# Summing the squares of three of the four RMS norms: on VectorE in SBUF, or on TensorE in PSUM

## The chip, the cores and the metric

One core of a Trainium2 chip runs the whole kernel. The metric is the device time of one execution in microseconds (us); the times are the median of three runs. The profile and the trace are those of one profiled execution.

## The reference

A decoder trunk of two layers over 256 tokens (T) and 2048 channels (D), all in f32. Layer 0 mixes by sliding-window attention, layer 1 by a gated linear recurrence (HGRN2). Both then run a squared-ReLU MLP of width 8192. There are four RMS norms over the channels, each followed by a shift and a scale from a conditioning vector:

```python
def rms_norm(x, gain):
    y = xf * lax.rsqrt(jnp.mean(xf * xf, axis=-1, keepdims=True) + EPS)
    return (y * gain.astype(jnp.float32)).astype(x.dtype)
...
    h = modulate(rms_norm(x, norm_mix[i]), sh1, sc1)
    ...
    x = x + g1[:, None, :] * y
    h = modulate(rms_norm(x, norm_mlp[i]), sh2, sc2)
    x = x + g2[:, None, :] * squared_relu_mlp(h, mlp_w1[i], mlp_w2[i])
```

## The kernel before, in words

**Layout.** The residual x lives in SBUF turned on its side: 16 blocks `X[kb]` of 128 channels (partitions) by 256 tokens. Each block is 128x256 f32. So the sum of squares of one token runs over all partitions of all 16 blocks.

**Matmuls.** Weights come in tiles of 1 MB (`raw`, five buffers, loaded by SyncE's queue at L212). ScalarE casts each half tile to a high part `wh` (L237), and VectorE subtracts to get the low part `wl` (L238), five buffers each. So up to four half tiles can be ready ahead of the one that TensorE is using. Activations are split in the same way into high and low parts. TensorE multiplies high by high, high by low and low by high. A product over 2048 channels is therefore 32 matmuls (two of 512 and 256 columns per block) or 48 (three of 256 columns per block, the "fold" form and the form `u`). All TensorE instructions are recorded at one line, L50, so they are told apart by their tiles: `mm` is a product, `ss` a sum of squares.

**The conditioning vectors.** The shifts, scales and gates are matrix-vector products. VectorE does most of them: one instruction per 1 MB tile at L226 (`raw<-raw,cond`), in an order that a list `seq` sets when the kernel is built, mixed with the weight tiles.

**The norms.** Norm one, at the start, runs over x as loaded. Norm two (before the MLP of layer 0), norm three (before the recurrence) and norm four (before the MLP of layer 1) run while the 16 blocks of x are being made: each time a block is ready (`resid` at L566 in attention and recurrence output, L942 in the last quarter of an MLP), `finish_x` puts a call of `norm_add` in a list of background work, and a `hook` between the matmuls calls it some matmuls later. `norm_add` squares the block on ScalarE (L470) into a tile `w` (three buffers), and later TensorE sums it over the partitions with a 32-column weight of ones. The four groups of 32 partitions of the PSUM tile `ss` take every fourth block. `pep` pins these matmuls behind the TensorE instruction in front of them. After the sixteenth, ScalarE copies `ss` to SBUF (L480).

**The end of a norm.** `norm_rstd` sums the copied tile over its partitions with two one-column matmuls (`sst`, with the column `quad` that is one in every 32nd row). It takes the reciprocal root on VectorE with small `nsm` instructions (L130 to L136, L492) and makes a diagonal `dg` (L497). `norm_bcast` spreads it over the partitions with one matmul `rb`, and ScalarE copies it to `rbs` (L505). Only then can `make_h` (L532 to L537) make the normed blocks H. Between x's last block and H, TensorE works on products of the not yet normed x (`u`, made at L549 to L551; the norm is multiplied in afterwards at L1008). At norms three and four there are three such products (`start_phase`), at norm two a larger number (`open_mlp`).

**Order.** A scheduler orders each engine's instructions when the kernel is built. On the chip each engine works through its own list in that order.

Of the kernel before, what the change touches and what calls it, by code (L numbers as in the profile page):

```python
# [7 lines left out]
F32 = mybir.dt.float32  # L8
F32R = mybir.dt.float32r
I32 = mybir.dt.int32  # L10
AF = mybir.ActivationFunctionType
ALU = mybir.AluOpType
AX = mybir.AxisListType

P = 128
T = 256
D = 2048
KB = 16
# [19 lines left out]


class Queue:  # L40
    """TensorE, with the name of its latest instruction; pinned instructions are issued behind that one."""

    def __init__(self, tc, engine, last, pin):
        self.tc, self.engine, self.last, self.pin = tc, engine, last, pin
# [17 lines left out]
def trunk(ctx, tc, a, out):  # L62
    nc = tc.nc
    dve, act, sp, pool_q = nc.vector, nc.scalar, nc.sync, nc.gpsimd
    last = []
    pe, pep = Queue(tc, nc.tensor, last, False), Queue(tc, nc.tensor, last, True)
# [4 lines left out]
    tmp = ctx.enter_context(tc.tile_pool(name="tmp", bufs=2))  # L71
    psum = ctx.enter_context(tc.tile_pool(name="psum", bufs=1, space=bass.MemoryType.PSUM))
# [5 lines left out]
    X = [xt[k // 4][:, k % 4, :] for k in range(KB)]  # L78
    col = iter(range(0, NCST))

    def part(n):
        c = next(col)
        for _ in range(n - 1):
            next(col)
        return cst[:, c:c + n]
# [4 lines left out]
    quad, kq, ogain = part(1), part(2), part(HG)  # L90
# [4 lines left out]
    ones = const.tile([P, P], F32, tag="ones", name="ones")  # L95
# [33 lines left out]
    def rsqrt(v, y, t, b):  # L129
        dve.tensor_scalar(out=y.bitcast(I32), in0=v.bitcast(I32), scalar1=-0.5,  # L130
                          scalar2=float(0x5F3759DF), op0=ALU.mult, op1=ALU.add)
        dve.tensor_scalar(out=b, in0=v, scalar1=-0.5, scalar2=None, op0=ALU.mult)
        for _ in range(3):
            dve.tensor_tensor(out=t, in0=y, in1=y, op=ALU.mult)
            dve.tensor_tensor(out=t, in0=t, in1=b, op=ALU.mult)
            dve.scalar_tensor_tensor(out=y, in0=t, scalar=1.5, in1=y, op0=ALU.add, op1=ALU.mult)  # L136
# [169 lines left out]
    def later(delay, fn):  # L306
        bg.append((bgst["slot"] + delay, bgst["n"], fn))
        bgst["n"] += 1
        bg.sort(key=lambda e: (e[0], e[1]))
# [144 lines left out]
    def wt(cols=T, name="w"):  # L454
        return tmp.tile([P, cols], F32, tag="w", name=name, bufs=3)
# [9 lines left out]

    nstate = {}

    def norm_add(kb, delay=0):
        sq = wt()
        act.activation(out=sq, in_=X[kb], func=AF.Square)  # L470
        if kb == 0:
            nstate["ss"] = psum.tile([P, T], F32, tag="pv", name="ss", bufs=1)
        g = slice((kb % 4) * 32, (kb % 4 + 1) * 32)

        def add():
            (pep if delay else pe).matmul(nstate["ss"][g, :], lhsT=ones[:, :32], rhs=sq,
                                          start=(kb < 4), stop=(kb >= 12))
            if kb == KB - 1:
                nstate["sc"] = wt()
                act.copy(out=nstate["sc"], in_=nstate["ss"])  # L480
        if delay:
            later(delay, add)
        else:
            add()

    def norm_rstd():
        ss = psum.tile([P, 2], F32, tag="sm", name="sst", bufs=1)
        for b in range(2):
            pe.matmul(ss[:, b:b + 1], lhsT=nstate["sc"][:, b * P:(b + 1) * P], rhs=quad,
                      start=True, stop=True)  # L490
        sm = tmp.tile([P, 8], F32, tag="nsm", name="nsm")
        dve.tensor_scalar(out=sm[:, 0:2], in0=ss, scalar1=1.0 / D, scalar2=EPS,  # L492
                          op0=ALU.mult, op1=ALU.add)
        rsqrt(sm[:, 0:2], sm[:, 2:4], sm[:, 4:6], sm[:, 6:8])
        dg = tmp.tile([P, T], F32, tag="dg", name="dg", bufs=1)
        for b in range(2):
            dve.tensor_scalar(out=dg[:, b * P:(b + 1) * P], in0=ident, scalar1=sm[:, 2 + b:3 + b],  # L497
                              scalar2=None, op0=ALU.mult)
        nstate["dg"] = dg

    def norm_bcast():
        rb = psum.tile([P, T], F32, tag="sm", name="rb", bufs=1)
        pe.matmul(rb, lhsT=ones, rhs=nstate["dg"], start=True, stop=True)
        rbs = tmp.tile([P, T], F32, tag="rbs", name="rbs", bufs=1)
        act.copy(out=rbs, in_=rb)  # L505
        return rbs

    def norm_finish():
        norm_rstd()
        return norm_bcast()  # L510

    gsc = const.tile([P, 4, KB], F32, tag="gsc", name="gsc")
# [33 lines left out]
    def make_u(l, half, kb):  # L546
        g = gsc[:, l * 2 + half, kb:kb + 1]
        u = optile(sets[0], kb)
        act.activation(out=u[:, :T], in_=X[kb], func=AF.Copy, scale=g)  # L549
        act.copy(out=u[:, T:T + 2], in_=ustate["sw"][:, kb, :].bitcast(F32))  # L550
        dve.scalar_tensor_tensor(out=u[:, T + 2:], in0=X[kb], scalar=g, in1=u[:, :T].bitcast(F32),  # L551
                                 op0=ALU.mult, op1=ALU.subtract)
        return u
# [15 lines left out]
    def evac_res(l, which, n):  # L569
        def f(ps):  # L570
            resid(l, which, n, ps)
            finish_x(n)
        return f
# [3 lines left out]
    def finish_x(n):  # L577
        if ustate["next"] is not None and n < ustate["lim"]:
            ustate["U"][n] = make_u(*ustate["next"], n)
        if n < KB - 1:  # L580
            later(2, lambda: norm_add(n, 2))
        elif ustate["next"] is None:
            norm_add(n)

    # layer 0: norm and modulation
    for k in range(KB):
        norm_add(k)
    rbs = norm_finish()
    feed = Feed(0, 0, rbs)
    feed.need(KH)  # L590
    H = feed.H
    ahead(LAG - 1)

    # layer 0: attention
    O = [None] * KB
    with tc.tile_pool(name="attn", bufs=2) as ap:
        dist = ap.tile([P, T], F32, tag="dist", name="dist", bufs=1)
# [239 lines left out]
    def open_mlp(mp, A, relu2):  # L837
# [5 lines left out]
        for n in range(2):  # L843
            finish_x(n)
# [10 lines left out]
        def s1():  # L855
            norm_rstd()
            later(NB, s2)
# [49 lines left out]
    def mlp_layer(l, H, last):  # L907
        mp_name = f"mlp{l}"
        with tc.tile_pool(name=mp_name, bufs=1) as mp:
# [20 lines left out]
            def evac2(c, n, fold):  # L930
                def f(ps):
                    if c == 0:
                        acc_tile(n)
                        total(ps, acc[n])
                        return
                    if not fold:
                        t = wt()
                        act.copy(out=t, in_=ps[:, T:])  # L938
                        dve.tensor_tensor(out=acc[n], in0=acc[n], in1=t, op=ALU.add)  # L939
                    dve.tensor_tensor(out=acc[n], in0=ps[:, :T], in1=acc[n], op=ALU.add)  # L940
                    if c == NCHUNK - 1:
                        dve.scalar_tensor_tensor(  # L942
                            out=X[n], in0=acc[n], scalar=mods[:, l, G2 * 16 + n: G2 * 16 + n + 1],
                            in1=X[n], op0=ALU.mult, op1=ALU.add)
                        if last:
                            act.dma_start(out=out[n], in_=X[n])
                        else:
                            finish_x(n)
                return f
# [32 lines left out]
    def start_phase(l, half, count, alloc, sink):  # L982
# [12 lines left out]
        def s1():  # L995
            norm_rstd()
            later(NB, s2)
# [21 lines left out]

    mlp_layer(0, None, False)  # L1020

    # layer 1: HGRN2
    hpool = ctx.enter_context(ExitStack())
    hp = hpool.enter_context(tc.tile_pool(name="hgrn", bufs=1))
    cmask = hp.tile([P, T], I32, tag="cmask", name="cmask")
# [281 lines left out]
```

## Time and profile before

| | |
|---|---|
| median of 3 runs | 2361.89 us (2360.89 to 2362.2) |
| span of the profiled execution | 2360.6 us, 1.3 us under the median |
| TensorE busy (matmuls) | 2294.6 us, 97% |
| VectorE busy | 1804.8 us, 76% |
| ScalarE busy | 1166.0 us, 49% |
| mean granted TensorE clock | 0.988 |
| HBM | 253 GB/s over the span |

The page gives busy times by engine, 40 slices of the span, the chain of work that ended last and the costliest groups of instructions. The profiled execution has no time of its own beside its span. In rows of the timeline the first number is the start in us, the second the duration. A number in square brackets at the end is the idle time of the engine in front of the row, and what ended it.

### The profile page before, as it was taken

To read this page: it belongs to the slowest core of one execution; us is meant where nothing else is said; L and a number is where in the kernel's file an instruction comes from. 1 tells how busy PE (TensorE), PEld (TensorE's weight loads), DVE (VectorE), ACT (ScalarE), POOL (GpSimd) and SP (SyncE) were. 2 spreads that over 40 slices of the span, in tenths; PEclk is the share of its full clock that TensorE was granted. 3 is DMA by queue.
4 is the path that set the end of the run, shared out by engine and by line. 5 is a ranking of instruction groups with operands and counts; after the bars stand their busy time and mean duration, and the time that the engine had idled before them with its cause. 6 is when DMAs were issued, how large, how long until landed. Compare 5 with 4: busy or idle time off the path is not lost.

```text
span 2360.6 us, 36968 instructions
## 1 busy us (share of the span) xinstructions
PE 2294.6 (97%) x14634; PEld 1992.4 (84%) x14634; DVE 1804.8 (76%) x3016; ACT 1166.0 (49%) x1977; POOL 3.5 (0%) x10
## 2 busy tenths in 40 slices
PE   2989999999999999999999999999999999999999
PEld 0985589998888888887888998999888888888888
DVE  8898777866888988986998888755865766665665
ACT  2435744544444444454665666644544444444443
POOL 0000000000000000000000000000000000000000
PEclk6999999999999999999999999999999999999999
DMA  9987788556989889874587777544666666555552
GB/s 381 339 307 305 285 322 322 192 187 241 322 333 338 322 325 336 320 289 161 198 299 257 265 268 268 196 158 160 219 229 235 248 216 249 198 194 181 194 191 95
DMA packets 84638, 598.80 MB, mean 254 GB/s; under 512 B 9456, under 2 KB 11504, under 8 KB 12272
## 3 DMA queue, kind: packets, MB, share of 16 engines
q1 hardware_dynamic: 81936, 593.81, 69.9%
q8 instruction: 115, 1.88, 0.3%
q10 hardware_dynamic: 2304, 2.10, 0.3%
q0 software_dynamic: 224, 0.52, 0.1%
q14 instruction: 59, 0.48, 0.1%
HBM read 594.04 MB, written 2.10 MB: 253 GB/s over the span
## 4 chain that ended last, share of the span: by engine, by line
PE 95%; DVE 3%; ACT 1%; DMA 1%; issue 0%; SPq 0%; ACTq 0%
PE mm L50 89%; DVE raw L226 2%; PE ss L50 1%; PE S L50 1%; PE A L50 1%; PE pv L50 1%; PE pt L50 1%; DVE wl L238 1%; PE on L50 0%; DMA raw<-in_mod_w_dram 0%; DMA x<-in_x_dram 0%; ACT wh L237 0%; DVE ht L532 0%; PE ssq L50 0%; PE sst L50 0%
## 5 line engine op out<-in xcount | busy, mean ns | idle before, releaser
L238 DVE TENSOR_TENSOR wl<-raw,wh 128x1024 fp32r<-128x1024 f32 x744 | 906.7, 1222 | 436.4 <-ACT wh L237 434.6
L237 ACT CAST wh<-raw 128x1024 fp32r<-128x1024 f32 x744 | 779.2, 1051 | 927.1 <-PE mm L50 836.6
L50 PE MATMUL mm<-h,wh 128*128 128x512 f32 (+2 forms) x3728 | 1154.1, 368 | 37.1 <-ACT wh L237 37.1
L50 PE MATMUL mm<-h,wl 128*128 128x256 f32 (+1 forms) x3232 | 907.0, 281 | 7.6 <-DVE wl L238 7.6
L50 PE MATMUL mm<-o,wh 128*128 128x512 f32 (+2 forms) x3120 | 863.1, 346 | 0.0
L50 PEld LDWEIGHTS mm<-h,wh 128*128 128x128 f32 x3728 | 671.4, 190 | 167.6 <-ACT wh L237 37.8
L50 PE MATMUL mm<-o,wl 128*128 128x256 f32 (+1 forms) x2432 | 679.6, 280 | 0.0
L50 PEld LDWEIGHTS mm<-h,wl 128*128 128x128 f32 x3232 | 612.5, 190 | 10.0 <-DVE wl L238 8.5
L50 PEld LDWEIGHTS mm<-o,wh 128*128 128x128 f32 x3120 | 538.1, 188 | 93.0 <-issue 10.4
L50 PEld LDWEIGHTS mm<-o,wl 128*128 128x128 f32 x2432 | 458.3, 189 | 0.4
L226 DVE CUSTOM_DVE_ANT_0 raw<-raw,cond 128x2048 f32<-128x2048 f32 x164 | 374.1, 2284 | 13.9 <-DMA raw<-in_mod_w_dram 10.4
L50 PE MATMUL mm<-wh,h 128*128 128x256 f32 x576 | 105.0, 283 | 1.3 <-ACT h L536 1.1
L50 PEld LDWEIGHTS mm<-wh,h 128*128 128x128 f32 x576 | 88.8, 189 | 2.2 <-ACT h L536 1.4
L50 PE MATMUL mm<-wl,h 128*128 128x256 f32 x288 | 81.0, 281 | 0.0
L459 ACT COPY w<-mm 128x256 f32<-128x256 f32 x186 | 67.6, 364 | 0.0
L463 ACT CAST h<-w 128x256 fp32r<-128x256 f32 x125 | 49.9, 404 | 28.9 <-DVE w L919 28.4
L50 PEld LDWEIGHTS mm<-wl,h 128*128 128x128 f32 x288 | 54.2, 188 | 0.5 <-issue 0.4
L919 DVE SCALAR_TENSOR_TENSOR w<-w 128x256 f32<-128x256 f32 x125 | 52.0, 421 | 2.2
L464 DVE TENSOR_TENSOR h<-w,h 128x256 fp32r<-128x256 f32 x125 | 51.5, 417 | 0.0
L460 DVE TENSOR_TENSOR w<-mm,w 128x256 f32<-128x256 f32 x109 | 45.5, 417 | 0.4 <-ACT w L459 0.2
L939 DVE TENSOR_TENSOR acc<-acc,w 128x256 f32<-128x256 f32 x94 | 39.4, 419 | 8.1 <-ACT w L938 8.0
L940 DVE TENSOR_TENSOR acc<-mm,acc 128x256 f32<-128x256 f32 x96 | 40.5, 422 | 6.5 <-PE mm L50 4.0
(193 smaller groups left out, 1113.2 us busy)
## 6 DMA issues: line engine op xcount, KB each, us to landing
raw<-in_mod_w_dram SPq DMA_DIRECT2D x164, 1024.0 KB, 5.9
raw<-in_mlp_dram SPq DMA_DIRECT2D x128, 1024.0 KB, 5.0
raw<-in_hin_dram SPq DMA_DIRECT2D x64, 1024.0 KB, 5.0
raw<-in_mlp1b_dram SPq DMA_DIRECT2D x64, 1024.0 KB, 4.9
raw<-in_mlp1a_dram SPq DMA_DIRECT2D x48, 1024.0 KB, 6.5
raw<-in_mod_g_dram SPq DMA_DIRECT2D x28, 1024.0 KB, 6.5
raw<-in_aout_dram SPq DMA_DIRECT2D x16, 1024.0 KB, 6.7
raw<-in_m1h_dram SPq DMA_DIRECT2D x16, 1024.0 KB, 4.9
```

Of the source, the lines that this page charges most:

```text
L50: r = fn(*args, **kw)
L226: dve.tensor_tensor_reduce(out=r, in0=r, in1=cond, scale=1.0, scalar=0.0, op0=ALU.mult, op1=ALU.add, accum_out=mods[:, e[1], e[2]:e[2] + 1])
L237: act.copy(out=wh, in_=part)
L238: dve.tensor_tensor(out=wl, in0=part, in1=wh.bitcast(F32), op=ALU.subtract)
L459: act.copy(out=t, in_=ps[:, T:])
L460: dve.tensor_tensor(out=out_t, in0=ps[:, :T], in1=t, op=ALU.add)
L463: act.copy(out=opt[:, :T], in_=src_t)
L464: dve.tensor_tensor(out=opt[:, T:2 * T], in0=src_t, in1=opt[:, :T].bitcast(F32), op=ALU.subtract)
L919: dve.scalar_tensor_tensor(out=t, in0=t, scalar=0.0, in1=t, op0=ALU.max, op1=ALU.mult)
L939: dve.tensor_tensor(out=acc[n], in0=acc[n], in1=t, op=ALU.add)
L940: dve.tensor_tensor(out=acc[n], in0=ps[:, :T], in1=acc[n], op=ALU.add)
```

## The change

For norms two to four, `norm_add` no longer uses TensorE. The square of block 0 is written by ScalarE straight into a tile `ssum` of 128x256 f32, in the slot of the tag `rbs`. Each of the other 15 blocks is squared into `w` as before, and VectorE adds it to `ssum`. At the end the two `sst` matmuls sum `ssum` over all its 128 rows, with a column of ones instead of `quad`. PSUM tile `ss`, its 48 matmuls and the three copies at L480 are gone from these norms. Norm one keeps its matmuls (`norm_first`); its copy goes to the tag `rbs` as well. Lines move down by two: L566 is L568, L532 is L534, L537 is L539, L497 is L499.

```diff
-    def norm_add(kb, delay=0):
+    def norm_add(kb):
+        if kb == 0:
+            nstate["ss"] = tmp.tile([P, T], F32, tag="rbs", name="ssum", bufs=1)
+            act.activation(out=nstate["ss"], in_=X[kb], func=AF.Square)
+            return
         sq = wt()
         act.activation(out=sq, in_=X[kb], func=AF.Square)
-        if kb == 0:
-            nstate["ss"] = psum.tile([P, T], F32, tag="pv", name="ss", bufs=1)
-        g = slice((kb % 4) * 32, (kb % 4 + 1) * 32)
-
-        def add():
-            (pep if delay else pe).matmul(nstate["ss"][g, :], lhsT=ones[:, :32], rhs=sq,
-                                          start=(kb < 4), stop=(kb >= 12))
-            if kb == KB - 1:
-                nstate["sc"] = wt()
-                act.copy(out=nstate["sc"], in_=nstate["ss"])
-        if delay:
-            later(delay, add)
-        else:
-            add()
+        dve.tensor_tensor(out=nstate["ss"], in0=nstate["ss"], in1=sq, op=ALU.add)
...
-    def norm_rstd():
+    def norm_rstd(sumcol=ones[:, :1]):
...
-            pe.matmul(ss[:, b:b + 1], lhsT=nstate["sc"][:, b * P:(b + 1) * P], rhs=quad,
+            pe.matmul(ss[:, b:b + 1], lhsT=nstate["ss"][:, b * P:(b + 1) * P], rhs=sumcol,
...
-            later(2, lambda: norm_add(n, 2))
+            later(2, lambda: norm_add(n))
```

TensorE in norm four, at the border between two products of the recurrence's output (`o` are the activations); before:

```order
L50 MATMUL mm<-o_15871,wh 128x256 x2
L50 MATMUL mm<-o_15871,wl 128x256
L50 MATMUL mm<-o_15884,wh 128x256 x2
L50 MATMUL mm<-o_15884,wl 128x256
L50 MATMUL ss<-w,ones 32x256
L50 MATMUL mm<-o_11910,wh 128x256 x2
L50 MATMUL mm<-o_11910,wl 128x256
```

The same place now:

```order
L50 MATMUL mm<-o_15863,wh 128x256 x2
L50 MATMUL mm<-o_15863,wl 128x256
L50 MATMUL mm<-o_15876,wh 128x256 x2
L50 MATMUL mm<-o_15876,wl 128x256
L50 MATMUL mm<-o_11902,wh 128x256 x2
L50 MATMUL mm<-o_11902,wl 128x256
```

The product's last matmul is now followed directly by the next product's first; the order around it is otherwise the same.

VectorE in norm four, one step of the same stretch (`x` is the residual, `h` the low part of `u`); before:

```order
L566 SCALAR_TENSOR_TENSOR x_74<-mm,mods,x_74 128x256
L238 TENSOR_TENSOR wl<-raw,wh 128x1024
L551 SCALAR_TENSOR_TENSOR h_16115<-x_74,gsc,h_16115 128x256
L238 TENSOR_TENSOR wl<-raw,wh 128x1024
L566 SCALAR_TENSOR_TENSOR x_74<-mm,mods,x_74 128x256
```

The same step now:

```order
L568 SCALAR_TENSOR_TENSOR x_74<-mm,mods,x_74 128x256
L238 TENSOR_TENSOR wl<-raw,wh 128x1024
L553 SCALAR_TENSOR_TENSOR h_16105<-x_74,gsc,h_16105 128x256
L486 TENSOR_TENSOR ssum<-ssum,w 128x256
L238 TENSOR_TENSOR wl<-raw,wh 128x1024
L568 SCALAR_TENSOR_TENSOR x_74<-mm,mods,x_74 128x256
```

The added instruction stands behind `h` and ahead of the second `wl`.

VectorE at the end of norm three, from the diagonal `dg` to the second normed block (`fl` are the first results of the recurrence's products, `ht` the first step of H); before:

```order
L497 TENSOR_SCALAR dg<-cst,nsm 128x128 x2
L238 TENSOR_TENSOR wl<-raw,wh 128x1024
L1008 TENSOR_TENSOR fl<-mm,rbs 128x256
L532 SCALAR_TENSOR_TENSOR ht<-x_73,gsc,rbs 128x256
L1009 TENSOR_SCALAR fl<-fl,swc 128x256
L532 SCALAR_TENSOR_TENSOR ht<-x_73,gsc,rbs 128x256
L368 TENSOR_REDUCE swc<-mm 128x1
L1008 TENSOR_TENSOR fl<-mm,rbs 128x256
L537 SCALAR_TENSOR_TENSOR h_11220<-ht,mods,h_11220 128x256
L1009 TENSOR_SCALAR fl<-fl,swc 128x256
L532 SCALAR_TENSOR_TENSOR ht<-x_73,gsc,rbs 128x256
L537 SCALAR_TENSOR_TENSOR h_11225<-ht,mods,h_11225 128x256
```

The same place now:

```order
L499 TENSOR_SCALAR dg<-cst,nsm 128x128 x2
L368 TENSOR_REDUCE swc<-mm 128x1
L238 TENSOR_TENSOR wl<-raw,wh 128x1024
L1008 TENSOR_TENSOR fl<-mm,rbs 128x256 x2
L1009 TENSOR_SCALAR fl<-fl,swc 128x256 x2
L534 SCALAR_TENSOR_TENSOR ht<-x_73,gsc,rbs 128x256 x2
L238 TENSOR_TENSOR wl<-raw,wh 128x1024
L226 ISA raw,mods<-raw,cond 128x2048
L226 ISA mods 128x1
L1060 TENSOR_SCALAR fl<-fl,om,lb 128x256 x2
L539 SCALAR_TENSOR_TENSOR h_11212<-ht,mods,h_11212 128x256
L1062 TENSOR_SCALAR kk<-fl 128x512
```

One more `wl`, one matrix-vector product (L226) and two instructions of L1060 now stand ahead of the first `h`. Between the `sst` matmuls and `dg` there are three `wl` now and two before. At the ends of norms two and four the orders of TensorE are the same but for the missing `ss` and one place of `sst`.

More of the change, by code (lines that the diff above doesn't have):

```diff
@@ L466, in trunk, with norm_first @@
     nstate = {}
-    def norm_add(kb, delay=0):
+    def norm_first():
+        ss = psum.tile([P, T], F32, tag="pv", name="ss", bufs=1)
+        for kb in range(KB):
+            sq = wt()
+            act.activation(out=sq, in_=X[kb], func=AF.Square)
+            g = slice((kb % 4) * 32, (kb % 4 + 1) * 32)
+            pe.matmul(ss[g, :], lhsT=ones[:, :32], rhs=sq, start=(kb < 4), stop=(kb >= 12))
+        nstate["ss"] = tmp.tile([P, T], F32, tag="rbs", name="ssum", bufs=1)
+        act.copy(out=nstate["ss"], in_=ss)
+        return norm_finish(quad)
+    def norm_add(kb):
+        if kb == 0:
+            nstate["ss"] = tmp.tile([P, T], F32, tag="rbs", name="ssum", bufs=1)
+            act.activation(out=nstate["ss"], in_=X[kb], func=AF.Square)
+            return
         sq = wt()
         act.activation(out=sq, in_=X[kb], func=AF.Square)
-        if kb == 0:
-            nstate["ss"] = psum.tile([P, T], F32, tag="pv", name="ss", bufs=1)
-        g = slice((kb % 4) * 32, (kb % 4 + 1) * 32)
-        def add():
-            (pep if delay else pe).matmul(nstate["ss"][g, :], lhsT=ones[:, :32], rhs=sq,
-                                          start=(kb < 4), stop=(kb >= 12))
-            if kb == KB - 1:
-                nstate["sc"] = wt()
-                act.copy(out=nstate["sc"], in_=nstate["ss"])
-        if delay:
-            later(delay, add)
-        else:
-            add()
-    def norm_rstd():
+        dve.tensor_tensor(out=nstate["ss"], in0=nstate["ss"], in1=sq, op=ALU.add)
+    def norm_rstd(sumcol=ones[:, :1]):
         ss = psum.tile([P, 2], F32, tag="sm", name="sst", bufs=1)
         for b in range(2):
-            pe.matmul(ss[:, b:b + 1], lhsT=nstate["sc"][:, b * P:(b + 1) * P], rhs=quad,
+            pe.matmul(ss[:, b:b + 1], lhsT=nstate["ss"][:, b * P:(b + 1) * P], rhs=sumcol,
                       start=True, stop=True)
@@ L506, in norm_bcast, with norm_finish @@
         return rbs
-    def norm_finish():
-        norm_rstd()
+    def norm_finish(sumcol):
+        norm_rstd(sumcol)
         return norm_bcast()
@@ L580, in finish_x @@
         if n < KB - 1:
-            later(2, lambda: norm_add(n, 2))
+            later(2, lambda: norm_add(n))
         elif ustate["next"] is None:
             norm_add(n)
-    for k in range(KB):
-        norm_add(k)
-    rbs = norm_finish()
+    rbs = norm_first()
     feed = Feed(0, 0, rbs)
```

## Prediction

> **What bounds the kernel now.** I read the page first: busy times, slices, chain.
>
> ```profile
> span 2360.6 us, 36968 instructions
> PE 2294.6 (97%) x14634; PEld 1992.4 (84%) x14634; DVE 1804.8 (76%) x3016; ACT 1166.0 (49%) x1977; POOL 3.5 (0%) x10
> PE   2989999999999999999999999999999999999999
> DVE  8898777866888988986998888755865766665665
> PE 95%; DVE 3%; ACT 1%; DMA 1%; issue 0%; SPq 0%; ACTq 0%
> ```
>
> After the first two slices TensorE has no free tenth, and the chain is 95% TensorE. VectorE is at 76% on the average but at 8 or 9 in many slices. So what leaves TensorE counts in full, unless VectorE or a transfer comes in its way there. The span is 1.3 us under the median of the runs, 2361.89; I carry the difference over to that median.
>
> Next, where the removed matmuls stand: the tile ss by stages (one window for each of norms two, three and four), then TensorE's own order of time in norm four.
>
> ```profile
> 250.00:450.00 200.00, 9.29 (x32) 2.06 (x32) 0.37 (x1) 1.00 0.78 284
> 1000.00:1200.00 200.00, 9.90 (x32) 2.20 (x32) 0.37 (x1) 1.00 0.64 228
> 1500.00:1700.00 200.00, 9.53 (x32) 2.21 (x32) 0.37 (x1) 1.00 0.50 174
> ```
>
> ```profile
> 1570.88 0.28 PE L50 MATMUL mm<-o,wl 128*128 128x256 f32 x1
> 1571.09 0.62 PE L50 MATMUL ss<-w,ones 128*32 128x256 f32 x2
> 1571.64 0.51 PE L50 MATMUL mm<-o,wh 128*128 128x256 f32 x2
> ...
> 1572.11 0.40 PE L50 MATMUL mm<-o,wh 128*128 128x256 f32 x2
> ...
> 1577.04 0.40 PE L50 MATMUL mm<-o,wh 128*128 128x256 f32 x2
> ...
> 1577.49 0.62 PE L50 MATMUL ss<-w,ones 128*32 128x256 f32 x2
> ```
>
> Each matmul of ss is two records, so 32 records are 16 matmuls, and their busy time is 9.3 to 9.9 us a norm, 28.7 in all. But busy time isn't what they cost. The product's triples (two high, one low) start every (1577.04 - 1572.11) / 14 = 0.352 us; 16 of them are 5.63 us. From one ss to the next it is 1577.49 - 1571.09 = 6.40 us. So one ss costs **0.77 us**: 0.21 instead of 0.12 us from the matmul ahead of it, 0.55 itself, and the first triple behind it takes 0.47 instead of 0.35.
>
> The same price from another side: the last quarter of the MLP has 32 matmuls of the same form a step in both layers, with ss in layer 0 and without in layer 1. The rows are VectorE's update of x, of layer 0 and then of layer 1.
>
> ```profile
> 1048.80 0.48 DVE L942 SCALAR_TENSOR_TENSOR x<-acc,mods,x 128x256 f32<-128x256 f32 x1
> ...
> 1099.55 0.48 DVE L942 SCALAR_TENSOR_TENSOR x<-acc,mods,x 128x256 f32<-128x256 f32 x1
> ```
>
> ```profile
> 2286.84 0.48 DVE L942 SCALAR_TENSOR_TENSOR x<-acc,mods,x 128x256 f32<-128x256 f32 x1
> ...
> 2342.84 0.48 DVE L942 SCALAR_TENSOR_TENSOR x<-acc,mods,x 128x256 f32<-128x256 f32 x1
> ```
>
> Eight steps of 6.344 us against ten of 5.600: **0.744 us** for one ss.
>
> **The change, part by part.** *Removed from TensorE.* Norms two and four: 2 x 16 x 0.77 = 24.6 us; norm three: 16 x 0.744 = 11.9; together 36.5 us, if nothing else is late. The nearest bound below is ss by itself, from its start to the next product's: 0.55 us, 26.4 for 48. I take 36.5, because the pitch holds the slower neighbours too.
>
> The Trainium skill, "TensorEngine Tiling (Array Packing)", section Tiling Modes, says that a change of tiling mode drains the array. The 0.21 and 0.47 us on either side of the 32-column matmul agree with that; by the rule the sum is the 36.5, without it the 26.4.
>
> *Removed from ScalarE.* Three copies at L480, 0.37 us each. They lie between the last ss and sst, beside running products, so nothing.
>
> *Added to VectorE.* 45 additions of 128x256 in SBUF. Layer 0's MLP has the same instruction:
>
> ```profile
> L939 DVE TENSOR_TENSOR acc<-acc,w 128x256 f32<-128x256 f32 x94 | 39.4, 419 | 8.1 <-ACT w L938 8.0
> ```
>
> That is 45 x 0.42 = 18.9 us on VectorE. Does it lie beside TensorE's work? The stages of norm two (two rows), three and four:
>
> ```profile
> 306.00:332.00 26.00, 26.00 (x210) 24.09 (x209) 23.99 (x33) 13.90 (x29) 0.00 (x0) 1.00 0.94 345
> 332.00:364.00 32.00, 32.00 (x252) 29.25 (x250) 27.01 (x33) 13.31 (x19) 0.00 (x0) 1.00 0.90 324
> 1060.00:1130.00 70.00, 70.00 (x396) 56.39 (x395) 46.07 (x69) 34.38 (x56) 0.18 (x1) 1.00 0.49 168
> 1600.00:1634.00 34.00, 34.00 (x269) 31.26 (x269) 17.26 (x21) 15.15 (x21) 0.00 (x0) 1.00 0.47 158
> ```
>
> The third busy number is VectorE. In norms three and four it is at 66% and 51%, and one addition a step leaves it under 80%: hidden. In norm two, four steps of 6.4 us hold 24.0 us of VectorE and the next five 27.0. With 0.42 more a step that is 25.7 and 29.1, against 22.5 and 28.2 for TensorE at 5.63 a step: VectorE is 4.1 us short. What covers it is how far it is ahead:
>
> ```profile
> ACT wh L237 <- PE mm L50: 30.0, 17, 2.2
> ```
>
> In 306 to 366 ScalarE's casts waited 17 times for TensorE to free a buffer, so the half tiles were full, up to four ahead of TensorE at 2.8 us each. A debt of 4.1 us fits into that, and the next stage has room. Transfers: 324 GB/s x 6.4 us are 2.1 MB a step, and a DMA share of 0.90 becomes 0.90 x 6.40 / 5.63 = 1.02, just at the limit. I take **1 us** of loss for norm two, between 0 and 4.1.
>
> Behind each addition on VectorE stands the next wl, and behind that the update of x that frees a PSUM tile. The addition waits for ScalarE's square, which comes right behind the cast of u, for whose low part the instruction ahead of the addition waits anyway:
>
> ```profile
> 1571.12 1.05 ACT L237 CAST wh<-raw 128x1024 fp32r<-128x1024 f32 x1 [1.75 <-PE mm L50]
> 1572.08 0.51 ACT L549 ACTIVATE h<-x,gsc 128x256 fp32r<-128x256 f32 x1
> 1572.49 0.40 ACT L470 ACTIVATE w<-x 128x256 f32<-128x256 f32 x1
> ```
>
> So it waits 0.3 to 0.4 us at most, where VectorE idles half of the time.
>
> *Moved: the end of norm three.* Here TensorE soon needs H, and H is what becomes late. VectorE, ScalarE and TensorE before:
>
> ```profile
> 1128.77 0.48 DVE L942 SCALAR_TENSOR_TENSOR x<-acc,mods,x 128x256 f32<-128x256 f32 x1
> 1135.11 2.28 DVE L226 CUSTOM_DVE_ANT_0 raw<-raw,cond 128x2048 f32<-128x2048 f32 x1
> 1137.59 1.23 DVE L238 TENSOR_TENSOR wl<-raw,wh 128x1024 fp32r<-128x1024 f32 x1
> 1142.87 0.47 DVE L537 SCALAR_TENSOR_TENSOR h<-ht,mods,h 128x256 fp32r<-128x256 f32 x1
> 1145.84 0.73 DVE L1060 TENSOR_SCALAR fl<-fl,om,lb 128x256 f32<-128x256 f32 x2
> ```
>
> ```profile
> 1140.65 0.37 ACT L505 COPY rbs<-rb 128x256 f32<-128x256 f32 x1 [0.78 <-PE rb L50]
> ```
>
> ```profile
> 1148.04 0.41 PE L50 MATMUL mm<-wh,h 128*128 128x256 f32 x2
> 1151.41 0.39 PE L50 MATMUL mm<-wh,h 128*128 128x256 f32 x1 [0.24 <-DVE h L537]
> 1154.32 0.39 PE L50 MATMUL mm<-wh,h 128*128 128x256 f32 x1 [1.09 <-ACT h L536]
> ```
>
> The last x is made at 1128.77, the first low part of H is ready at 1143.34, and TensorE takes it at 1148.04: a cover of 4.7 us. Two ss lie in between, so TensorE arrives 2 x 0.744 = 1.5 us sooner, and 3.2 us are left. In the new order one more wl (1.2 us) lies ahead of dg; without ss and its copy the chain starts sooner, so about 1 us stays. Another wl, a matrix-vector product and L1060 stand ahead of the first H: 1.2 + 2.2 + 0.7 = 4.1. H is some 5 us later against 3.2 of cover: a stall of about 2 us, and the later blocks, which wait for VectorE too, add about 1. So the 1.5 us of two ss are lost, and some 3 us more (between 0 and 5): **4.5 us**. The ends of norms two and four keep their order; the sum is ready when sst comes, so nothing.
>
> *Sum.* 36.5 - 1 - 4.5 = 31.0 us; 2361.9 - 31.0 = **2331 us**.
>
> **The rivals.** *The end of norm three costs only its two ss, and norm two nothing.* 2361.9 - 36.5 + 1.5 = 2327. For it: TensorE was full right to these places. Against: the moved matrix-vector product. It goes with the forecast's mechanism; 15%.
>
> *Only ss itself comes back.* If the slow neighbours belong to the product's border, as they would with the change of PSUM tile, 26.4 - 5.5 = 21 us: 2341. Against it stands layer 1's pitch of 5.600 with the same borders; 12%.
>
> *Slower: the addition holds VectorE's list.* If the square stood on ScalarE behind a cast that waits for TensorE, the addition, the wl behind it and x's update would wait with it: 1.75 us (the row above) and 1.05 for the cast. It decides once the four half tiles are used up; then 45 x 2.8 = 126 us against 36.5, or 2451; if it holds in one norm of the three, 42 against 36.5: 2367. The squares' place behind the cast of u speaks against it; 3%.
>
> The Trainium skill, "TensorE: Matmul & The Clock Gate", section "Architectural detail: the array is 16× 32×32, not 1× 128×128", says that VectorE and ScalarE work strictly in order. That is the rule by which this rival would come about; the trace agrees where it was read: the product at 1135.11 and the wl at 1137.59 stand as in the list.
>
> *Nothing comes of it.* The 0.744 us is another difference between the layers, and VectorE takes the rest: within 0.2%, 2362; 3%.
>
> **How the numbers follow.** The forecast has 67%: 2331, by its own bounds 2327 (no loss beyond the two ss) to 2336 (4.1 and 6.5 us lost). The range takes in the rivals on both sides of it: 2324 (the first with 0.05 us more for each ss) to 2343 (the second with 2 us more lost at the ends). A measurement of this kernel tells about 0.2%, 4.7 us, from no change. Faster by more than that: 67 + 15 + 12 = 94%, of which I give 1 to mishaps: 93%; within it 3%, with 1 of the mishaps 4%; slower 3%.
>
> **What would show it.** The steps of x's update in the last quarter of layer 0's MLP come every 5.6 us instead of 6.344, and triples in norm four run on without a break, at 5.63 a step. TensorE's busy time falls by about 34: the 31 us and some 3 of new idle time. The addition takes 0.42 us and no TensorE row names it as releaser, apart perhaps from sst. At the end of norm three TensorE waits for h some 4 us in all instead of 1.33. The forecast is wrong if the pitch stays above 5.8 (the price of ss, or VectorE), if TensorE waits for wl between 306 and 364 by more than 4 us, or if the end of norm three waits more than 8.

## The result, and the profile after

| | before | after |
|---|---|---|
| median | 2361.68 us (2360.89 to 2362.2) | **2334.05 us** (2333.61 to 2335.32) |
| span of the profiled execution | 2360.6 us | 2332.5 us |
| ratio of the medians | | 0.9884, interval 0.987 to 0.9898 |

The medians are now of four runs each. The kernel became 27.6 us faster; the forecast was 31, its range reached from 2324 to 2343. The profiled executions differ by 28.1 us, and the ledger below is made of them.

First the page of the kernel after: the sums, and the group of matmuls that use the first blocks of H.

```profile
PE 2263.7 (97%) x14538; PEld 1986.2 (85%) x14538; DVE 1818.7 (78%) x3061; ACT 1166.8 (50%) x1974; POOL 3.5 (0%) x10
L50 PE MATMUL mm<-wh,h 128*128 128x256 f32 x576 | 106.5, 284 | 4.2 <-DVE h L539 2.7
```

TensorE has 96 records less (48 matmuls) and is busy 30.9 us less; VectorE has 45 instructions more (median 0.42 us each in the trace, as forecast) and is busy 13.9 us more; that is less than 45 x 0.42 = 18.9, because rows that follow directly on one another overlap by some 0.1 us (a row of two `h` of 0.48 us each takes 0.86). TensorE, at 97%, still bounds the kernel. New is in the second line: TensorE waits 4.2 us for H, where the same group waited 1.3 before.

To see where the 28.1 us come from, I cut both executions at the same instructions. TensorE before (`gt` opens the stretch of norm two, `rb` is the matmul that spreads a norm, `tp` the first transpose of the recurrence, `ot` one of its last):

```profile
305.85 0.33 PE L50 MATMUL gt<-cst,w 128*128 128x128 f32 x1 [0.27 <-ACT w L254]
312.54 0.62 PE L50 MATMUL ss<-w,ones 128*32 128x256 f32 x4
313.09 0.51 PE L50 MATMUL mm<-o,wh 128*128 128x256 f32 x2
433.71 0.59 PE L50 MATMUL rb<-dg,ones 128*128 128x256 f32 x2
1174.02 0.27 PE L50 MATMUL tp<-cst,kd 128*128 128x128 f32 x1
1546.92 0.33 PE L50 MATMUL ot<-cst,ob 128*128 128x128 f32 x1 [0.17 <-ACT ob L1153]
1644.16 0.59 PE L50 MATMUL rb<-dg,ones 128*128 128x256 f32 x2
```

TensorE after:

```profile
306.92 0.33 PE L50 MATMUL gt<-cst,w 128*128 128x128 f32 x1 [0.27 <-ACT w L254]
423.64 0.59 PE L50 MATMUL rb<-dg,ones 128*128 128x256 f32 x2
1157.66 0.27 PE L50 MATMUL tp<-cst,kd 128*128 128x128 f32 x1
1530.05 0.33 PE L50 MATMUL ot<-cst,ob 128*128 128x128 f32 x1 [0.18 <-ACT ob L1153]
1611.49 0.58 PE L50 MATMUL sst<-ones,ssum 128*128 128x1 f32 x4 [0.15 <-DVE ssum L486]
1616.21 0.59 PE L50 MATMUL rb<-dg,ones 128*128 128x256 f32 x2
```

VectorE after: two updates of x in the last quarter of layer 0's MLP, the last update of norm three (1108.28) with the product and the first low part of H behind it; then two updates in norm four.

```profile
1037.97 0.48 DVE L942 SCALAR_TENSOR_TENSOR x<-acc,mods,x 128x256 f32<-128x256 f32 x1
...
1099.57 0.48 DVE L942 SCALAR_TENSOR_TENSOR x<-acc,mods,x 128x256 f32<-128x256 f32 x1
...
1108.28 0.48 DVE L942 SCALAR_TENSOR_TENSOR x<-acc,mods,x 128x256 f32<-128x256 f32 x1
...
1125.73 2.28 DVE L226 CUSTOM_DVE_ANT_0 raw<-raw,cond 128x2048 f32<-128x2048 f32 x1
...
1128.59 0.48 DVE L539 SCALAR_TENSOR_TENSOR h<-ht,mods,h 128x256 fp32r<-128x256 f32 x1
```

```profile
1546.19 0.48 DVE L568 SCALAR_TENSOR_TENSOR x<-mm,mods,x 128x256 f32<-128x256 f32 x1 [0.57 <-PE mm L50]
...
1608.38 0.48 DVE L568 SCALAR_TENSOR_TENSOR x<-mm,mods,x 128x256 f32<-128x256 f32 x1 [0.57 <-PE mm L50]
```

| stretch | before | after | gain |
|---|---|---|---|
| start to `gt` | 305.85 | 306.92 | -1.07 |
| norm two: `gt` to `rb` | 127.86 | 116.72 | +11.14 |
| `rb` to the last x of norm three | 695.06 | 684.64 | +10.42 |
| last x to the first `tp`: end of norm three | 45.25 | 49.38 | -4.13 |
| `tp` to `ot`: recurrence | 372.90 | 372.39 | +0.51 |
| norm four: `ot` to `rb` | 97.24 | 86.16 | +11.08 |
| `rb` to the end of the span | 716.44 | 716.29 | +0.15 |
| sum | | | 28.10 |

The three gains are close to whole numbers of one price: 15 x 0.744 = 11.16, 14 x 0.744 = 10.42, 15 x 0.744 = 11.16. The x updates now come every (1099.57 - 1037.97) / 11 = 5.600 us, as in layer 1, and the steps of norm four every (1608.38 - 1546.19) / 11 = 5.654. Norms two and four have 16 `ss` each but give back 15 prices: the row at 312.54 holds two of them (x4, four records), and the next product starts 0.55 us later, as behind a single one.

The loss lies where the forecast put it, at the end of norm three. TensorE there:

```profile
1126.95 0.38 PE L50 MATMUL mm<-wh,h 128*128 128x256 f32 x1 [0.54 <-ACT h L538]
1129.13 0.39 PE L50 MATMUL mm<-wh,h 128*128 128x256 f32 x1 [1.79 <-DVE h L539]
1131.86 0.39 PE L50 MATMUL mm<-wh,h 128*128 128x256 f32 x1 [0.94 <-ACT h L538]
1133.84 0.38 PE L50 MATMUL mm<-wh,h 128*128 128x256 f32 x1 [0.92 <-DVE h L539]
```

And the same place in windows of 2 us: length, TensorE's busy time, then the granted clock.

```profile
1126.00:1128.00 2.00, 0.80 (x5) 1.00 0.61 127
1128.00:1130.00 2.00, 0.87 (x7) 1.00 0.99 418
1130.00:1132.00 2.00, 1.06 (x8) 1.00 1.01 422
1132.00:1134.00 2.00, 1.08 (x5) 1.00 0.20 82
1134.00:1136.00 2.00, 2.00 (x12) 0.59 0.00 0
1136.00:1138.00 2.00, 2.00 (x10) 0.56 0.00 0
1138.00:1140.00 2.00, 2.00 (x17) 1.00 0.03 8
```

The waits are 4.19 us, against 1.33 before. But a second cost stands right behind them, and I had not forecast it: the clock granted to TensorE falls to 0.59 and 0.56 for two windows. That is 2 x 0.41 + 2 x 0.44 = 1.70 us of work lost. In windows of half a microsecond the clock reads 0.50 throughout from 1134.5 to 1137.5. The first low part of H begins 1128.59 - 1108.28 = 20.3 us after the last x; before it was 1142.87 - 1128.77 = 14.1.

### The profile page after: what moved, and what is told of

It is laid out like the page before. It is cut to its first block, busy times and chain, and to the rows that moved or that the text cites. A ratio compares the mean times of both kernels' runs of the same rounds, so it can differ in the third digit from the quotient of the medians.

```text
span 2332.5 us, 36840 instructions
## 1 busy us (share of the span) xinstructions
PE 2263.7 (97%) x14538; PEld 1986.2 (85%) x14538; DVE 1818.7 (78%) x3061; ACT 1166.8 (50%) x1974; POOL 3.5 (0%) x10
## 4 chain that ended last, share of the span: by engine, by line
PE 94%; DVE 4%; DMA 1%; ACT 1%; issue 1%; ACTq 0%; DVEq 0%
PE mm L50 89%; DVE raw L226 2%; DVE wl L238 1%; PE S L50 1%; PE A L50 1%; PE pv L50 1%; PE pt L50 1%; DMA raw<-in_mod_w_dram 1%; PE on L50 0%; PE cb L50 0%; ACT wh L237 0%; PE ss L50 0%; DVE ht L534 0%; PE ssq L50 0%; PE sst L50 0%
## 5 line engine op out<-in xcount | busy, mean ns | idle before, releaser
L226 DVE CUSTOM_DVE_ANT_0 raw<-raw,cond 128x2048 f32<-128x2048 f32 x164 | 374.4, 2286 | 15.6 <-DMA raw<-in_mod_w_dram 11.5
```

The lines of the kernel that those rows point to most:

```text
L226: dve.tensor_tensor_reduce(out=r, in0=r, in1=cond, scale=1.0, scalar=0.0, op0=ALU.mult, op1=ALU.add, accum_out=mods[:, e[1], e[2]:e[2] + 1])
```

## The experiments

**Theory.** One `ss` costs TensorE 0.744 us, itself and its neighbours; the additions on VectorE are hidden; what is lost at the end of norm three comes from the new order of VectorE, which puts a matrix-vector product and a `wl` ahead of H. **Rivals:** the additions themselves cost something; the end of norm three would be lost in any kernel without `ss`; the price comes from the change of PSUM tile, or is only the two passes of an f32 matmul.

### Is the addition hidden?

Each of the 45 additions gets a second one whose result is not read (it overwrites the used square):

```diff
         dve.tensor_tensor(out=nstate["ss"], in0=nstate["ss"], in1=sq, op=ALU.add)
+        dve.tensor_tensor(out=sq, in0=nstate["ss"], in1=sq, op=ALU.add)
```

> The changed kernel with a second addition of the same size, whose result nobody reads, behind each of the 45: 18.9 us more on VectorE. Theory (the additions lie beside TensorE's work): norms three and four take no longer, norm two, where VectorE is short, 0 to 3 us: 2334 to 2337 us. Rival (VectorE is at its limit where the additions stand): 2353 us.

Measured: 2333.31 us (2330.55 to 2334.66), ratio to before 0.9878 (0.9865 to 0.9892). That is not above the kernel after, so 45 x 0.42 = 18.9 us more on VectorE cost nothing that can be told. The trace says it more sharply than the medians, whose interval is some 3 us wide: from `gt` to the end of the span this execution takes 2025.1 us, with single additions 2025.6. It is even true of norm two, where I had feared 1 us: from `gt` at 303.50 to `rb` at 420.21 it is 116.71 us, as with single additions (116.72).

### Norm three alone back on TensorE

The changed kernel, with `norm_add` of before for norm three only:

```diff
+        if nstate["n"] != 3:
+            norm_add_dve(kb)
+            return
...
+            (pep if delay else pe).matmul(nstate["pss"][g, :], lhsT=ones[:, :32], rhs=sq,
+                                          start=(kb < 4), stop=(kb >= 12))
```

> Norms two and four as changed, norm three with its matmuls as before. Theory (48 matmuls at 0.744 us each come back, and 4 to 6 us of it are given back at the end of norm three, because H is made later there): norms two and four bring 11.1 us each, norm three only 6: 2361.7 - 22 = 2339.5 us, and TensorE waits for H at the end of norm three as before, 1.33 us. Rival (the missing microseconds are spread over the three norms, 9.2 each): 2343.3 us.

Measured: 2340.51 us (2338.73 to 2341.35), ratio 0.9909 (0.9896 to 0.9923). So norm three's change is worth 6.5 us net. Its 16 `ss` are 11.9 us, so about 5.4 are lost at its end; the forecast's 7.4 net was a little too much. TensorE waits 1.35 us for H there, about as before (1.33).

### The products later

The end of norm three waits for a matrix-vector product at L226 on VectorE, one of those of layer 1's second norm. In `seq` they are mixed with the recurrence's weights. Here they come later:

```diff
     put([a["hin"][i] for i in range(64)], two(1, SC2, SH2, 0, KB),
-        per=lambda i: max(0, i - 4) * 32 // 56)
+        per=lambda i: max(0, i - 12) * 32 // 48)
```

> The changed kernel, with the matrix-vector products of layer 1's second norm loaded and computed from the 13th weight tile of the recurrence on instead of the 5th, so that none of them (2.3 us each on VectorE) lies at the end of norm three. Theory (these products ahead of H on VectorE are what TensorE waits for): the waits for H fall from 4.2 us to at most 1, and the time to 2330.5 us (2329 to 2332). Rival (H is late because TensorE comes 1.5 us sooner and the sum is later, the products only stand there): 2334 us, within 0.5.

> The kernel before with the same later place of the matrix-vector products. Theory (before, H was in time but for 1.33 us, and one later wait of 1.24 us hung on such a product): 2359 to 2361 us. Rival (the later place is worth 3 us or more by itself, with the sums on TensorE too): 2358.5 us or less.

Measured: the changed kernel with it 2329.22 us (2328.04 to 2329.76), ratio 0.9862 (0.9848 to 0.9875); the kernel before with it 2361.88 (2361.1 to 2362.69), ratio 1.0002 (0.9993 to 1.0011). So 4.8 us come back, and only where the new order stands; the 1 to 3 us that I had expected in the kernel before did not come. From the last x to the `ot` the profiled execution takes 416.93 us, against 421.77 in the kernel after. VectorE's last x and first low part of H in this kernel, then TensorE's waits:

```profile
1107.72 0.48 DVE L942 SCALAR_TENSOR_TENSOR x<-acc,mods,x 128x256 f32<-128x256 f32 x1
...
1119.51 0.48 DVE L539 SCALAR_TENSOR_TENSOR h<-ht,mods,h 128x256 fp32r<-128x256 f32 x1
```

```profile
1129.74 0.38 PE L50 MATMUL mm<-wh,h 128*128 128x256 f32 x1 [0.23 <-DVE h L539]
...
1131.93 0.39 PE L50 MATMUL mm<-h,wl 128*128 128x256 f32 x1 [1.10 <-DVE wl L238]
```

H comes 11.8 us after the last x instead of 20.3, and the waits for it are 0.23 us; a new wait of 1.10 us, for a `wl`, is left. The clock stays at 1.00 here.

### The last square straight to TensorE

In the changed kernel VectorE no longer adds the square of block 15; `sst` takes it with two more one-column matmuls into the same sums:

```diff
+        if kb == KB - 1:
+            nstate["last"] = sq
+            return
         dve.tensor_tensor(out=nstate["ss"], in0=nstate["ss"], in1=sq, op=ALU.add)
...
+                pe.matmul(ss[:, b:b + 1], lhsT=last[:, b * P:(b + 1) * P], rhs=sumcol,
+                          start=False, stop=True)
```

> The changed kernel, but the square of the last block (15) of norms two to four is not added by VectorE: sst takes it as a second pair of one-column matmuls into the same two sums. Theory (the last addition is ready when sst comes, and what is late at the end of norm three is H behind the products moved ahead of it): VectorE's 0.36 us at the end of norm three fall away, TensorE gets two more one-column matmuls a norm, some 0.3 to 0.5 us, 1 to 1.5 us in all: 2334 to 2336. Rival (the addition itself delays the norm's chain, and this is part of the 5.8 us lost at the end of norm three): sst starts about 0.4 us sooner, H with it, and the time is below 2333.

> The changed kernel with the later products of layer 1's second norm (12 and 48 in place of 4 and 56) and with the last square taken by sst. Theory: as the later products alone, 2329.2, plus the 1 to 1.5 us of the additional one-column matmuls: 2329.5 to 2331. Rival (with the products out of the way the addition is what H waits for next): 2328 or less.

Measured: alone 2329.92 us (2329.32 to 2331.41), ratio 0.9866 (0.9851 to 0.9881); with the later products 2328.85 (2328.5 to 2330.3), ratio 0.9862 (0.9847 to 0.9877). The first one contradicts what I expected: 4.1 us faster than the kernel after, where the theory had said up to 2 slower. (The intervals of the two ratios overlap a little; in the traces, the last x to the `ot` is 418.60 us against 421.77.) The rival's number came true, but not by the 0.4 us of the addition. VectorE:

```profile
1108.34 0.48 DVE L949 SCALAR_TENSOR_TENSOR x<-acc,mods,x 128x256 f32<-128x256 f32 x1
...
1121.40 0.47 DVE L546 SCALAR_TENSOR_TENSOR h<-ht,mods,h 128x256 fp32r<-128x256 f32 x1
```

H comes 13.1 us after the last x, 7.2 sooner than in the kernel after. One instruction less made the scheduler choose another order: no second product at L226 stands ahead of H any more (the next one is at 1146.46). So this run too removes the late H, by another way, and with the products already later it adds nothing that can be told (2328.85 against 2329.22; neither of the two expectations, 2329.5 to 2331 and 2328 or less, was met).

### The clock behind the waits

TensorE alone gets 26 matmuls more, whose result nobody reads, at the places of the three long waits; VectorE's order is that of the kernel after.

```diff
+            for j in range(q[0]):
+                pep.matmul(fil["t"], lhsT=fil["o"], rhs=wh[:, c], start=True, stop=True)
...
+            for j in range(q[1]):
+                pep.matmul(fil["t"], lhsT=o[:, hs], rhs=wh[:, c], start=True, stop=True)
...
+                fil["n"] = {0: (0, 12), 2: (7, 7)}
```

> The changed kernel, VectorE's order unchanged, with 26 matmuls of the product's form whose result nobody reads, on TensorE alone: 12 between the high and the low part of the first block of H at the end of norm three, 7 ahead of the third block and 7 between its parts, about 0.12 us each, 3.1 us in all, at the three places where TensorE waits 1.79, 0.94 and 0.92 us. Theory (of what the end of norm three costs, 1.7 us is the clock, which is granted at 0.50 for 3.4 us behind these waits): the granted clock stays at 1.00 up to the first tp, H comes no sooner, and the time is 1.2 to 1.8 us below 2334.05 of the changed kernel: 2332.2 to 2332.9, although TensorE does more. Rival (the clock falls for another reason, or costs nothing): the clock falls as before, and the time is 2334 or above.

Measured: 2332.65 us (2331.09 to 2333.02), ratio 0.9876 (0.9859 to 0.9892). The same windows, and the first twelve fillers:

```profile
1126.00:1128.00 2.00, 1.46 (x12) 1.00 0.40 66
1128.00:1130.00 2.00, 1.64 (x14) 1.00 0.94 397
1130.00:1132.00 2.00, 2.00 (x18) 1.00 1.02 418
1132.00:1134.00 2.00, 1.81 (x13) 1.00 0.37 156
1134.00:1136.00 2.00, 1.78 (x13) 1.00 0.07 20
```

```profile
1127.56 1.59 PE L50 MATMUL fil<-wh,h 128*128 128x256 f32 x12
```

H comes as late as before (20.3 us after the last x), TensorE does more, and yet the profiled execution needs 1.85 us less from the last x to the same `ot` (419.92 us instead of 421.77), and 1.57 us less from `gt` to the end of the span. The clock stays at 1.00. So the fall behind the waits came from TensorE's idleness, and it cost about what the windows said; a wait of 0.6 us for `qa` further on, which is gone too, and 0.3 us more of waiting for a `wh` account for most of the difference. In the medians it is 1.4 us, but the intervals of the two ratios overlap; the place in the trace is the stronger evidence. The other traces fit: with doubled additions, where TensorE waits 3.0 us for H at the same place, the clock falls as well (0.82 and 0.75 in windows of 4 us), and where it waits 1.3 to 1.4 us there (the kernel before, norm three on TensorE, the last square by `sst`) it stays at 1.00.

### What makes one `ss` dear

Four versions of the kernel before. In the first, the ones have 128 columns instead of 32, so every `ss` writes the whole tile (and the mean divides by 4 D). In the second, squares and ones are moreover in rounded f32, the form of the products. In the third and fourth each `ss` is done twice with a weight of a half, into the same 32 rows or into the next 32 rows. In the kernel before `norm_add` makes norm one as well, so these versions change its 16 `ss` too; that lies in the first 20 us, and the stage in front of `gt` ends between 303.9 and 307.7 us in them, which is within its scatter (see below).

```diff
-            (pep if delay else pe).matmul(nstate["ss"][g, :], lhsT=ones[:, :32], rhs=sq,
+            (pep if delay else pe).matmul(nstate["ss"], lhsT=ones, rhs=sq,
```

```diff
+        sq = tmp.tile([P, T], F32R, tag="w", name="sq", bufs=3)
...
+            (pep if delay else pe).matmul(nstate["ss"], lhsT=onesr, rhs=sq,
```

```diff
+            for r in range(2):
+                (pep if delay else pe).matmul(nstate["ss"][g, :], lhsT=half[:, :32], rhs=sq,
```

```diff
+            for r in range(2):
+                j = (kb + r) % 4
+                g = slice(j * 32, (j + 1) * 32)
```

> The kernel before, with a weight of 128 columns of ones instead of 32, so that every matmul of ss fills the whole array and none changes its tiling (each of the 128 rows then holds the full sum; sst's scale is a quarter). If the change of tiling is what makes ss dear (0.21 us ahead of it and 0.12 more behind it), a matmul costs some 0.45 us instead of 0.744: 2348 us. If it is the step from the products' rounded f32 to full f32 with two passes, it costs as rb does, 0.64 us by the trace of before: 2357 us.

> As the run with 128 columns of ones, and the squares and ones in the products' rounded f32, so the sums of squares are made from squares rounded to that format. If two passes and the change of format are the price, a matmul of ss now costs what one of the product does, 0.12 us: 48 x 0.62 less, 2332 us, or 2333 if norm three's end is a little worse. If most of the 0.744 us is the stop between two products, whatever stands there, 2350 us or more.

> The kernel before with every matmul of ss twice into the same 32 rows, with ones of a half. If the second one runs after the first, it costs its two passes, about 0.45 us each: 48 x 0.45 = 22 us, 2383 us; if it costs the whole price again, 0.744 us: 2397 us; nothing if ss were hidden: 2362 us.

> The same with the second matmul into the next 32 rows of ss. Theory (matmuls into two different groups of 32 columns run side by side, as the first two of norms two and four do in the trace of before, in 0.55 us together): 2362 to 2365 us. Rival (each has its price, wherever it writes): as with the same group, 2383 us.

| version | time, us | ratio to before |
|---|---|---|
| 128 columns | 2346.8 (2346.05 to 2347.42) | 0.9936 (0.9921 to 0.9951) |
| 128 columns, rounded f32 | 2333.68 (2332.89 to 2334.47) | 0.9881 (0.9866 to 0.9895) |
| twice, same rows | 2381.8 (2380.97 to 2382.66) | 1.0084 (1.0069 to 1.0099) |
| twice, next rows | 2362.61 (2361.97 to 2363.75) | 1.0003 (0.9993 to 1.0013) |

VectorE's updates of x in norm three, eleven steps apart, with 128 columns and then with 128 columns in rounded f32:

```profile
1049.06 0.48 DVE L941 SCALAR_TENSOR_TENSOR x<-acc,mods,x 128x256 f32<-128x256 f32 x1
...
1115.27 0.48 DVE L941 SCALAR_TENSOR_TENSOR x<-acc,mods,x 128x256 f32<-128x256 f32 x1
```

```profile
1044.28 0.48 DVE L943 SCALAR_TENSOR_TENSOR x<-acc,mods,x 128x256 f32<-128x256 f32 x1
...
1107.09 0.48 DVE L943 SCALAR_TENSOR_TENSOR x<-acc,mods,x 128x256 f32<-128x256 f32 x1
```

One `ss` and the next product in norm four, in the order of the table:

```profile
1559.15 0.59 PE L50 MATMUL ss<-w,ones 128*128 128x256 f32 x2
1559.39 0.59 PE L50 MATMUL mm<-o,wh 128*128 128x256 f32 x2
```

```profile
1560.79 0.28 PE L50 MATMUL ss<-sq,onesr 128*128 128x256 f32 x1
1560.91 0.40 PE L50 MATMUL mm<-o,wh 128*128 128x256 f32 x2
```

```profile
1571.41 1.05 PE L50 MATMUL ss<-w,half 128*32 128x256 f32 x4
1572.39 0.51 PE L50 MATMUL mm<-o,wh 128*128 128x256 f32 x2
```

```profile
1559.66 0.63 PE L50 MATMUL ss<-w,half 128*32 128x256 f32 x4
1560.22 0.51 PE L50 MATMUL mm<-o,wh 128*128 128x256 f32 x2
```

From its start to the next product's, `ss` takes 0.24 us over 128 columns, 0.12 in rounded f32, 0.98 twice in the same rows and 0.56 twice in two groups of rows, against 0.55 with 32 columns. That leaves out the neighbours; the pitch, the time from one step to the next, has them. A step of norm three is 6.344 us with 32 columns, 66.21 / 11 = 6.019 with 128, 62.81 / 11 = 5.710 in rounded f32 and 5.600 without `ss`. So of the 0.744 us some 0.32 belong to the 32 columns, 0.31 to the full f32, and 0.11 are what any matmul of the product costs. In the whole time it is 15.2 us for the columns and another 13.1 for the rounded form; in the profiled executions, from `gt` on, 13.5 and 15.2. Neither is the dear part alone.

The doubled `ss` shows what kind of price the columns have. A second one into the same 32 rows costs 0.43 us more, no more than one over 128 columns (6.019 - 5.600 = 0.42). So the 0.32 us are paid once for a visit to the 32 columns, not for each matmul in it. `rb`, which I had put at 0.64 us, agrees too: in the trace of before it is 0.24 us to the next product's start and makes the triple behind it 0.19 longer, 0.43 in all. And the rounded `ss` writes another PSUM tile between two products as before and costs 0.11, so the change of PSUM tile is not the price.

So the kernel with rounded 128-column `ss` on TensorE (2333.68) is as fast as the change (2334.05), without any addition on VectorE, but it sums squares that are rounded to that format. And two `ss` into different groups of rows cost as much as one, which is why 16 matmuls of norms two and four gave back 15 prices.

### Would any kernel without the price lose the end of norm three?

The rounded version, which keeps the order of before at that place, with the later products:

```diff
-        per=lambda i: max(0, i - 4) * 32 // 56)
+        per=lambda i: max(0, i - 12) * 32 // 48)
```

> The kernel before with the ss matmuls over all 128 columns and in rounded f32 (2333.7 without more), and with the later products of layer 1's second norm. Theory (the later products pay where VectorE's new order put a matrix-vector product ahead of the first block of H; here the order is that of before, and TensorE waits for H only 1.34 us): no change, 2333 to 2334.5. Rival (the later products pay in any kernel whose ss no longer holds TensorE up at that place): 2329 to 2331.

Measured: 2333.23 us (2331.84 to 2334.06), ratio 0.9877 (0.9861 to 0.9894), against 2333.68 without. No change, although the waits for H are gone: TensorE waits for `qa` instead, 1.8 us where it was 0.7. In the rounded version without the later products TensorE already waits only 1.34 us for H, as before, with the clock at 1.00; H comes 13.2 us after the last x. The loss belongs to the order that came with the change, not to the missing `ss`.

## Why the prediction was right, and where its sum was off

The direction, the mechanism and the place of the loss were as forecast; the sum was 3 us too good.

- *Price of one `ss`.* I took 0.77 for norms two and four and 0.744 for norm three. All three gave 0.74 (11.14 / 15, 10.42 / 14 and 11.08 / 15); the 0.77 came from a triple of 0.352 us worked out over 4.93 us, and the step of norm four is 5.654, not 5.63. Of the 48, two pairs run side by side. Removed is 46 x 0.744 = 34.2 instead of 36.5: **-2.3**. I had summed the busy records and overlooked the row with x4.
- *Only ss itself comes back* (2341): falls. The slow neighbours went with it, at every norm. The Trainium skill, "TensorEngine Tiling (Array Packing)", section Tiling Modes, says that a change of tiling mode drains TensorE. The runs agree for a part of the price: with 128 columns a step is 0.32 us shorter, and a second `ss` in the same mode does not pay these 0.32 again. The other part, 0.31 us, is the full f32, which the prediction did not set apart.
- *Norm two, 1 us lost* (between 0 and 4.1): nothing was lost, **+1**. TensorE waits for no half tile in 306.92 to 423.64 (its busy time there is the whole stretch), and a second addition changes nothing. The half tiles ahead were cover enough.
- *The end of norm three, 4.5 us lost.* It was **5.1**: from the last x to the `ot` 418.15 us before, 416.66 without the two `ss` in it, and 421.77 after. The size is near, but its parts were wrong. H came 6.2 us later, where I had said some 5, and the waits grew by 2.9 us, as forecast ("some 4 us in all"). But the 1.5 us of "lost" `ss` that I added to them were a double count: TensorE came sooner by them, and that was in the waits already. Missing was the clock, 1.7 us, which by chance stands in their place: 2.9 + 1.7, and 0.5 that I have not traced. That 4.5 came so near is luck in this part.
- *Slower, the addition holds VectorE's list* (2451 or 2367): falls. The one row of TensorE that names an addition is `sst` at 1611.49, with 0.15 us, as forecast.
- *TensorE's busy time* fell by 30.9, not by 34. Its idle time grew by 2.8 us (66.0 to 68.8), near the 3 of the forecast; what is missing is the 2.9 us by which the sum was too good.
- *Not in the sum:* the first stage ended 1.07 us later. Its end lies between 303.5 and 307.7 in the other profiles of this study (303.5 to 307.3 in those that leave norm one alone), whatever was changed in the norms behind it, so I take it for scatter. It is not part of the change.

34.2 - 5.1 - 1.07 + 0.15 (the rest of the span) = 28.2, against 28.1.

## What to carry to other kernels

Price an instruction by the pitch of the loop around it, and count rows that hold two of them: a small matmul of another form cost 0.744 us among products of 0.12, more than its own record, but two in different row groups cost no more than one. Before moving such work to another engine, try its cheap form where it stands: here the full width and the rounded type together gave the same gain without a new instruction on VectorE, at the price of rounded squares. And when a change makes the scheduler write a new order, look at the next point where the bounding engine waits: the late block of H cost its waits and the slow clock behind them, and moving a background product (2329.22 us) won both back.

## What the runs showed of the hardware

- TensorE's granted clock fell to half at the end of a stretch of 8 us in which it was busy only 3.81 us (four windows), for about 3.4 us (1.70 us lost at 0.50), although the longest single wait was 1.79 us. With the waits filled it stayed at 1.00. The Trainium skill, "TensorE: Matmul & The Clock Gate", Part 1, has half clock after an idle window of about 3.4 us and full clock after a busy one. The length agrees; that a stretch with work in it was enough does not follow from its words. It can also come with less: in the run with the last square taken by `sst`, one wait of 1.33 us, for `qa` at 1451.73 to 1453.06, with no other wait from 1440 on, has slow windows behind it:

```profile
1452.00:1456.00 4.00, 2.94 (x28) 0.86 1.01 371
1456.00:1460.00 4.00, 4.00 (x21) 0.72 0.34 109
```

  while the waits for H in the kernel before, 0.24 and 1.09 us in 1150 to 1156, left it at 1.00. Where the border lies, these runs do not tell.
- Behind an f32 `ss` into 32 rows (a weight of 32 columns, 256 tokens), a second one costs 0.43 us when it goes into the same 32 rows (0.98 - 0.55) and 0.01 when it goes into the next 32 rows (0.56 - 0.55). Over the full 128 columns an f32 `ss` costs 0.42 us by the pitch, a rounded one 0.11.
- VectorE can be all but full without holding TensorE up. In the first part of norm two after the change it is busy 30.47 of 31.08 us (third busy number), and TensorE all the time:

```profile
306.92:338.00 31.08, 31.08 (x264) 31.08 (x265) 30.47 (x42) 18.61 (x35) 0.00 (x0) 1.00 0.94 328
```
